# A hybrid decoder block: the SSD skip factors are loaded as one row per partition, and their column layout is formed on chip

## The chip, the cores and the metric

The kernel runs on one core of a Trainium2 chip. The metric is the device time of one execution in microseconds. A core has a matrix engine (PE), a vector engine (DVE), a scalar engine (ACT), a general engine (POOL) and a sync engine (SP), which here issues nearly all transfers. Each engine works through its own list of instructions in order, and an instruction that has to wait for another engine or for a transfer holds back everything behind it on its engine.

## The reference

One layer of a decoder for 512 tokens of width 1024, all in float32. After an RMSNorm, one projection of 11512 columns feeds three token mixers side by side: a sparse attention with a learned index (DSA), a three-way attention (NSA) and a state-space mixer (SSD). Their outputs are gated, mixed, projected and added to the input; a feed-forward block with squared ReLU follows.

```python
h = rms_norm(x, norm1_g)
u = h @ w_in
(dq, dk, dv, iq, ik, iw, nq, nkv, ng, sz, sxbc, sdt, mg) = split(u)
y_a, y_b, y_c = dsa(dq, dk, dv, iq, ik, iw), nsa(nq, nkv, ng), ssd(sz, sxbc, sdt)
x = x + (sig(g_A) * (y_a @ W_A) + sig(g_B) * (y_b @ W_B) + sig(g_C) * (y_c @ W_C)) @ w_out
x = x + square(relu(rms_norm(x, norm2_g) @ w_ff1)) @ w_ff2
```

The change touches one small constant, `ssd_d`: 32 skip factors, one for each head of the SSD. In the mixer they enter as

```python
y = y_diag + y_off + xs * d_skip.reshape(SSD_GROUPS, SSD_HPG)[:, :, None]
```

where `xs` has 32 heads of 64 channels, 2048 channels in all.

## The kernel before

A float32 product is made from split operands: each matrix is written as a high part in a reduced format and the remainder (`hTh` and `hTl` for the normalised input, `whi` and `wlo` for weights), and three matrix products are added (lines 458, 459 and 460). So every weight block goes through the same steps: SP loads 128x1024 floats into one of three buffers `wraw` (line 154), ACT makes `whi` (line 173), DVE or POOL makes `wlo` (line 175), which frees the `wraw` buffer for the next load, and PE uses both.

The start of the program matters here. The four token tiles of `x` are loaded, normalised, transposed on PE (line 427) and split into `hTh` by ACT (line 437) and `hTl` by DVE (line 438). While later tiles are still being made, PE begins the first projection, `c0`, 456 columns wide: for each token tile 24 products (lines 458 to 460), written to `pj` for tiles 0 and 1 and to `sc` for tiles 2 and 3. The transposes of token tiles 2 and 3 stand in the middle of this stream. The transposes of a tile write a buffer named `pT`, of which there are two; one is free again when line 438 has read it. The projection after `c0` is `nkv`, whose first four weight blocks are 128x1024.

Small constants are loaded by `const_load` (from line 322), which is called after token tile 1 of `c0` (line 705). A helper `wide` loads a row of n values once for each of the 128 partitions; `put` does the same into a tile that exists already, as for `dtb` and `alog`, the 32 step biases and decay logs of the SSD. The skip factors were different: the tile `dcol` has 128 partitions and 16 columns, and its element at partition p and column m is the factor of the head to which channel 128 m + p belongs, head 2m for p below 64 and head 2m + 1 above. It was filled by two loads, one for each half of the partitions, each taking every second of the 32 values (line 344), and halved in place on DVE (line 345). `const_cols` (from line 349) transposes other constants on PE and copies them; it is called after token tile 1 of `nkv` (line 742). `dcol` is first read by ACT in `conv`, line 860, when the SSD inputs are projected.

The order of the instructions on each engine is not that of the code: a scheduler places them by the order in which they are written, priorities, and a simulated timeline of its own. So an instruction that is written inside `const_load` can stand on DVE between two steps of the normalisation.

## Time and profile before

| what | value |
|---|---|
| median of 3 runs | 1374.2 us (1374.09 to 1375.94) |
| time of the profiled execution | 1373.8 us |
| its span, first to last instruction | 1372.1 us |
| mean granted clock of PE | 0.988 of full speed |
| PE busy | 1334.8 us, 97% of the span |
| DVE busy | 995.5 us, 73% |
| ACT busy | 727.6 us, 53% |
| POOL busy | 269.9 us, 20% |

The times in the prediction that come from the trace are counted from the start of the span. An engine counts as busy while it works on an instruction, not while it waits. In a line of the timeline the first two numbers are the start and the duration, then come the engine and the line of the program, what is written and from what, the shape, and in brackets the time that the engine sat idle before and what ended the wait. `SPq` is the queue of SP, where issuing a transfer is shown; when the data has landed stands in the view of the transfers. In the chain of waits each row is a start, a duration and what the end of the program was held by at that time.

### The profile page before, as it was taken

How to read it: one execution, taken by the hardware profiler on the slowest of the kernel's cores; microseconds unless marked ns; L12 is line 12 of the kernel's file. 1: busy time of each engine (PE TensorE's matmuls, PEld its weight loads, DVE VectorE, ACT ScalarE, POOL GpSimd, SP SyncE). 2: the span in 40 equal slices, each digit the busy share in tenths (PEclk: the TensorE clock that was granted, in tenths of full speed). 3: DMA queues.
4: the chain of work that ended last, by engine and by line, in shares of the span. 5: the costliest groups of instructions: out<-in, count | busy, mean ns of one | idle time of the engine just before them, and what ended most of it. 6: DMA issues, size and time to landing. Idle time of an engine off the chain costs nothing.

```text
span 1372.1 us, 19609 instructions
## 1 busy us (share of the span) xinstructions
PE 1334.8 (97%) x6827; PEld 1113.0 (81%) x6827; DVE 995.5 (73%) x1970; ACT 727.6 (53%) x1393; POOL 269.9 (20%) x242
## 2 busy tenths in 40 slices
PE   6899999999999999999999999999999999999998
PEld 5788888888887777888888888787879888888887
DVE  4469997788987767457768798979745666767741
ACT  4355525577777776347666655656334344444430
POOL 2135201111005667600000021113001201102000
PEclk8899999999999999999999999999999999999999
DMA  4335655555559999564336453434535655746531
GB/s 141 99 116 144 163 161 150 152 135 155 143 145 327 304 276 318 181 176 119 112 113 180 119 152 117 147 119 144 193 94 168 129 165 125 182 114 130 151 123 50
DMA packets 253713, 213.73 MB, mean 156 GB/s; under 512 B 17817, under 2 KB 205101, under 8 KB 253614
## 3 DMA queue, kind: packets, MB, share of 16 engines
q1 hardware_dynamic: 237644, 188.88, 45.9%
q0 software_dynamic: 15232, 20.98, 8.1%
q10 hardware_dynamic: 738, 2.63, 0.5%
q8 instruction: 54, 0.88, 0.3%
q14 instruction: 45, 0.37, 0.1%
HBM read 171.74 MB, written 40.70 MB: 155 GB/s over the span
## 4 chain that ended last, share of the span: by engine, by line
PE 82%; DMA 7%; DVE 6%; ACT 2%; issue 2%; POOL 1%; SPq 0%; DVEq 0%; ACTq 0%; POOLq 0%
PE pj L458 19%; PE pj L459 19%; PE pj L460 19%; PE sc L460 3%; PE sc L459 3%; PE sc L458 3%; PE pT L983 2%; DMA dcol<-in_ssd_d_dram 2%; PE sc L924 2%; PE sc L923 2%; PE pv L995 2%; PE pv L996 1%; PE sc L1311 1%; DMA yr<-yc_d 1%; DMA E<-ac_d 1%
## 5 line engine op out<-in xcount | busy, mean ns | idle before, releaser
L173 ACT ACTIVATE whi<-wraw 128x1024 fp32r<-128x1024 f32 (+2 forms) x190 | 198.3, 1047 | 256.9 <-PE pj L459 136.8
L175 DVE TENSOR_TENSOR wlo<-wraw,whi 128x1024 fp32r<-128x1024 f32 (+1 forms) x176 | 223.3, 1273 | 99.6 <-ACT whi L173 99.2
L458 PE MATMUL pj<-hTh,whi 128*128 128x512 f32 x512 | 203.7, 398 | 2.3 <-DVE cacc L852 2.0
L460 PE MATMUL pj<-hTh,wlo 128*128 128x512 f32 x512 | 202.6, 396 | 0.0
L459 PE MATMUL pj<-hTl,whi 128*128 128x512 f32 x512 | 202.4, 395 | 0.0
L932 ACT ACTIVATE p<-p,nb,rs 128x256 f32<-128x256 f32 (+3 forms) x160 | 107.8, 676 | 34.2 <-DVE nb L930 34.1
L458 PEld LDWEIGHTS pj<-hTh,whi 128*128 128x128 f32 x512 | 96.7, 189 | 21.8 <-ACT eab L1340 2.2
L460 PEld LDWEIGHTS pj<-hTh,wlo 128*128 128x128 f32 x512 | 96.7, 189 | 18.9 <-issue 0.2
L459 PEld LDWEIGHTS pj<-hTl,whi 128*128 128x128 f32 x512 | 96.5, 189 | 18.5 <-issue 0.2
L458 PE MATMUL pj<-yh,whi 128*128 128x512 f32 (+1 forms) x288 | 106.1, 373 | 4.1 <-ACT yh L828 3.1
L459 PE MATMUL pj<-yl,whi 128*128 128x512 f32 (+1 forms) x288 | 107.2, 372 | 0.1
L460 PE MATMUL pj<-yh,wlo 128*128 128x512 f32 (+1 forms) x288 | 106.1, 368 | 0.0
L459 PE MATMUL pj<-h2l,whi 128*128 128x512 f32 (+1 forms) x256 | 96.3, 376 | 0.0
L460 PE MATMUL pj<-h2h,wlo 128*128 128x512 f32 (+1 forms) x256 | 96.2, 376 | 0.0
L458 PE MATMUL pj<-h2h,whi 128*128 128x512 f32 (+1 forms) x256 | 96.1, 376 | 0.0
L458 PE MATMUL pj<-whi,hTh 128*128 128x512 f32 (+2 forms) x208 | 81.4, 391 | 3.2 <-DVE v_s L560 2.2
L460 PE MATMUL pj<-whi,hTl 128*128 128x512 f32 (+2 forms) x208 | 80.6, 388 | 0.0
L459 PE MATMUL pj<-wlo,hTh 128*128 128x512 f32 (+2 forms) x208 | 80.1, 385 | 0.0
L1042 POOL DMA_DIRECT2D qu<-q_d x32 | 23.6, 738 | 272.4 <-PE sc L924 165.5
L987 ACT ACTIVATE pth<-pT 128x512 fp32r<-128x512 f32 x95 | 54.9, 593 | 32.1 <-PE pT L983 28.6
L458 PE MATMUL sc<-whi,fh 128*128 128x512 f32 x168 | 65.4, 389 | 0.0
L459 PE MATMUL sc<-wlo,fh 128*128 128x512 f32 x168 | 65.4, 389 | 0.0
(408 smaller groups left out, 3159.5 us busy)
## 6 DMA issues: line engine op xcount, KB each, us to landing
wraw<-in_w_in_dram SPq DMA_DIRECT2D x84, 512.0 KB, 3.9
wraw<-in_w_ff_dram SPq DMA_DIRECT2D x58, 512.0 KB, 4.1
qd<-in_w_ff_dram POOLq DMA_DIRECT2D x18, 512.0 KB, 5.8
gld<-g_d SPq DMA_DIRECT2D x35, 256.0 KB, 2.7
q_d<-qev SPq DMA_DIRECT2D x64, 128.0 KB, 3.3
qu<-q_d POOLq DMA_DIRECT2D x32, 256.0 KB, 3.6
E<-ac_d SPq DMA_DIRECT2D x16, 512.0 KB, 6.7
xz<-xzt_d SPq DMA_DIRECT2D x16, 512.0 KB, 5.2
```

What stands on the lines that cost most here:

```text
L173: act.activation(hi[:, :m], r[:, :m], AF.Copy)
L175: (pool if i in LOWP else dve).tensor_tensor(lo[:, :m], r[:, :m], f(hi[:, :m]), op=ALU.subtract)
L458: pe.matmul(o, lh, rh, start=first, stop=False)
L459: pe.matmul(o, lh, rl, start=False, stop=False)
L460: pe.matmul(o, ll, rh, start=False, stop=last)
L923: pe.matmul(s_[:, h % w, :n], u.q[h], kh[:, :n], start=True, stop=False)
L924: pe.matmul(s_[:, h % w, :n], u.q[h], kl[:, :n], start=False, stop=True)
L932: act.activation(u.p[h][:, :n], u.p[h][:, :n], AF.Exp, bias=u.nb[:, h:h + 1], scale=rs8[:, u.b, u.h0 + h:u.h0 + h + 1], accum_out=u.sm[:, ...
L983: pe.transpose(pt[:, h], u.p[h][:, kb * 128:kb * 128 + 128], ident)
L987: act.activation(ph, ptf, AF.Copy)
L995: pe.matmul(o, vk, ph0, start=st, stop=False)
L1042: pool.dma_start(q.rearrange("p (i a) c -> p i (a c)", i=2), src)
```

## The change

The two strided loads of `dcol` and the halving in place go away. `const_load` loads the 32 factors as one contiguous row for every partition into a new tile `dsk`, as `wide` does for other constants. `const_cols` gets two DVE instructions, one for each half of the partitions: each reads every second column of `dsk`, multiplies by 0.5 and writes the 16 columns of `dcol`. The values in `dcol` are the same as before.

```diff
--- before.py
+++ after.py
@@ -340,9 +340,7 @@
         rows("posr", A["nsa_cmp_pos"], 64, 64)
         put(dtb, A["ssd_dt_bias"], 32)
         put(alog, A["ssd_a_log"], 32)
-        for e in range(2):
-            nc.sync.dma_start(dcol[64 * e:64 * e + 64], dram(A["ssd_d"], e, [[0, 64], [2, 16]]))
-        dve.tensor_scalar(dcol, dcol, 0.5, None, op0=ALU.mult)
+        wide("dsk", A["ssd_d"], 32)
         dve.tensor_tensor(g_dsa, CL["gq_d"], CL["gk_d"], op=ALU.mult)
         dve.tensor_tensor(g_nsa, CL["gk_n"].rearrange("p (a b) -> p a b", b=64), bc(CL["gq_n"][:, None, :], [128, 3, 64]), op=ALU.mult)
 
@@ -354,6 +352,9 @@
         pe.transpose(p[:, 184:200], CL["rows3"], ident[:16, :16])
         dve.tensor_copy(convc, p[:, 0:120])
         dve.tensor_copy(gcol, p[:, 184:200])
+        for e in range(2):
+            r = slice(64 * e, 64 * e + 64)
+            dve.tensor_scalar(dcol[r], CL["dsk"].rearrange("p (m e) -> p m e", e=2)[r, :, e], 0.5, None, op0=ALU.mult)
         pv_ = p[:64, 120:184].rearrange("p (v a l) -> p v a l", v=2, l=2)
         dve.tensor_copy(pos2[0:64], pv_[:, :, :, 0])
         dve.tensor_copy(pos2[64:128], pv_[:, :, :, 1])
```

How the lists of the engines read at the two places concerned, with line numbers of each kernel's own text (from `const_cols` on, a line of the changed kernel has a number higher by one). First DVE, at the end of the normalisation, before the change; `x_125` and `x_126` are token tiles 2 and 3, `wlo` 128x912 the last weight block of `c0`, and what stands after "waits" are the counters on which the instruction waits (those beginning with DMA are transfers).

```order
L438 TENSOR_TENSOR hTl<-pT,hTh 128x4x128 [waits Activation_49] x2
L412 SCALAR_TENSOR_TENSOR x_125<-x_125,rs_168,sc 128x512 [waits DMAHW3_49,Pool_49]
L412 SCALAR_TENSOR_TENSOR x_126<-x_126,rs_168,sc 128x512 [waits DMAHW4_49,Pool_49]
L175 TENSOR_TENSOR wlo<-wraw,whi 128x912 [waits DMAHW2_49,DMAHW1_49,Activation_49]
L345 TENSOR_SCALAR dcol<-dcol 128x16 [waits DMAHW3_49,DMAHW2_49]
L438 TENSOR_TENSOR hTl<-pT,hTh 128x4x128 [waits Activation_49] x2
L175 TENSOR_TENSOR wlo<-wraw,whi 128x1024 [waits DMAHW6_49,Activation_49]
```

The same place of DVE with the change:

```order
L439 TENSOR_TENSOR hTl<-pT,hTh 128x4x128 [waits Activation_49] x2
L413 SCALAR_TENSOR_TENSOR x_125<-x_125,rs_168,sc 128x512 [waits DMAHW3_49,Pool_49]
L413 SCALAR_TENSOR_TENSOR x_126<-x_126,rs_168,sc 128x512 [waits DMAHW4_49,Pool_49]
L175 TENSOR_TENSOR wlo<-wraw,whi 128x912 [waits DMAHW2_49,DMAHW1_49,Activation_49]
L357 TENSOR_SCALAR dcol<-dsk 64x16 [waits DMAHW2_49]
L357 TENSOR_SCALAR dcol<-dsk 64x16
L439 TENSOR_TENSOR hTl<-pT,hTh 128x4x128 [waits Activation_49] x2
L175 TENSOR_TENSOR wlo<-wraw,whi 128x1024 [waits DMAHW6_49,Activation_49]
```

Although the code has the two new instructions in `const_cols`, the scheduler puts them where the one instruction stood: one is replaced by two, and the first of them waits for one transfer in place of two.

Then the transfers of SP around the skip factors, before the change:

```order
L324 DMA posr<-in_nsa_cmp_pos_dram 64x64 [waits DMAHW7_49]
L324 DMA dtb<-in_ssd_dt_bias_dram 128x32 [waits DMAHW0_49]
L324 DMA alog<-in_ssd_a_log_dram 128x32 [waits DMAHW1_49]
L344 DMA dcol<-in_ssd_d_dram 64x16x1 [waits DMAHW2_49]
L344 DMA dcol<-in_ssd_d_dram 64x16x1 [waits DMAHW3_49]
L154 DMA wraw<-in_w_in_dram 128x2x512 [waits DMAHW4_49,DVE_49]
L154 DMA wraw<-in_w_in_dram 128x2x512 [waits DMAHW5_49,DVE_49]
```

And with the change:

```order
L324 DMA posr<-in_nsa_cmp_pos_dram 64x64 [waits DMAHW7_49]
L324 DMA dtb<-in_ssd_dt_bias_dram 128x32 [waits DMAHW0_49]
L324 DMA alog<-in_ssd_a_log_dram 128x32 [waits DMAHW1_49]
L324 DMA dsk<-in_ssd_d_dram 128x32 [waits DMAHW2_49]
L154 DMA wraw<-in_w_in_dram 128x2x512 [waits DMAHW3_49,DVE_49]
L154 DMA wraw<-in_w_in_dram 128x2x512 [waits DMAHW4_49,DVE_49]
```

Two transfers become one in the same place, with the shape of the one for `alog`. The two rows after it are the second and third weight blocks of `nkv`. Apart from these places, the engines' lists hold the same instructions in the same order.

## The prediction

> **What bounds the kernel now.** I read the page first: which engine is full, and in which slices it is not.

> ```profile
> span 1372.1 us, 19609 instructions
> PE 1334.8 (97%) x6827; PEld 1113.0 (81%) x6827; DVE 995.5 (73%) x1970; ACT 727.6 (53%) x1393; POOL 269.9 (20%) x242
> PE   6899999999999999999999999999999999999998
> ```

> PE is busy for 97% of the span; only the first two slices of 34 us are visibly short. What PE lacks is 1372.1 - 1334.8 = 37.3 us, and the waits of PE, summed over the whole run, say where most of it lies:

> ```profile
> PE pT L427 <- DVE hTl L438: 15.4, 1, 15.4
> PE pj L458 <- ACT yh L828: 3.1, 3, 1.2
> PE pj L458 <- DVE v_s L560: 2.2, 1, 2.2
> ```

> One single wait, the transposes of token tile 3 waiting for DVE, holds 15.4 us; the next cause has 3.1 us in three pieces. The chain of waits over the first 60 us follows it back:

> ```profile
> 17.60 22.15 DMA dcol<-in_ssd_d_dram
> ...
> 39.85 0.17 DVE dcol L345
> 40.02 0.60 DVE hTl L438
> 40.63 0.04 issue
> 40.67 1.12 PE pT L427 x4
> ```

> The transposes start when DVE has split the transposed tile 2; DVE does that when it has halved `dcol`; and that waits for the second strided load of `dcol`, issued at 17.60 and landed 22.15 us later, at 39.75. The DVE timeline shows what queues behind this wait, the ACT timeline when its next input was there:

> ```profile
> 20.79 1.10 DVE L175 TENSOR_TENSOR wlo<-wraw,whi 128x912 fp32r<-128x912 f32 x1
> 39.85 0.17 DVE L345 TENSOR_SCALAR dcol<-dcol 128x16 f32<-128x16 f32 x1 [17.96 <-DMA dcol<-in_ssd_d_dram]
> 39.93 1.28 DVE L438 TENSOR_TENSOR hTl<-pT,hTh 128x512 fp32r<-128x512 f32 x2
> ```

> ```profile
> 22.36 1.08 ACT L437 ACTIVATE hTh<-pT 128x512 fp32r<-128x512 f32 x2 [2.77 <-PE pT L427]
> ```

> DVE is free at 21.89 and idle for 17.96 us. The `hTl` instructions behind the wait need only `hTh`, whose two halves ACT had written by 23.44. So a constant that nobody reads before the SSD projections stops the normalisation, and through it PE.

> **The change part by part.** *The stall on PE.* These rows of PE's timeline carry the sum:

> ```profile
> 17.59 0.37 PE L458 MATMUL pj<-whi,hTh 128*128 128x456 f32 x1
> 20.08 0.36 PE L458 MATMUL pj<-whi,hTh 128*128 128x456 f32 x1
> 21.73 1.03 PE L427 MATMUL pT<-ident,x 128*128 128x128 f32 x8
> 22.52 0.46 PE L459 MATMUL pj<-wlo,hTh 128*128 128x456 f32 x1
> 24.89 0.36 PE L459 MATMUL sc<-wlo,hTh 128*128 128x456 f32 x1
> 40.67 1.12 PE L427 MATMUL pT<-ident,x 128*128 128x128 f32 x4 [15.42 <-DVE hTl L438]
> 46.15 0.90 PE L427 MATMUL pT<-ident,x 128*128 128x128 f32 x4
> 46.80 0.45 PE L460 MATMUL sc<-whi,hTl 128*128 128x456 f32 x1
> 53.92 0.39 PE L458 MATMUL pj<-whi,hTh 128*128 128x512 f32 x1
> 54.15 0.40 PE L459 MATMUL pj<-wlo,hTh 128*128 128x512 f32 x1
> ```

> Products overlap, so I count from start to start. From 17.59 to 20.08 lie 12 products: 2.49 us, 0.21 each. The last product before the stall starts at 24.89, so the next instruction could have started at 25.10. It started at 40.67: **15.57 us**.

> *The slow restart.* After the stall PE is not at full speed. The granted clock, in stretches:

> ```profile
> 27.00:28.00 1.00, 0.00 (x0) 0.00 (x0) 0.00 (x0) 0.00 (x0) 0.00 (x0) 1.00 0.05 0
> 30.00:40.60 10.60, 0.00 (x0) 0.00 (x0) 0.75 (x3) 0.00 (x0) 0.00 (x0) 0.50 0.24 77
> 45.00:46.00 1.00, 1.00 (x4) 0.88 (x3) 0.00 (x0) 0.00 (x0) 0.00 (x0) 0.50 0.10 37
> 47.00:48.00 1.00, 1.00 (x7) 0.91 (x6) 0.28 (x1) 0.92 (x4) 0.00 (x0) 1.00 0.00 0
> ```

> (The seventh number is the clock.) It was still 1.00 at 27 to 28, is 0.50 from 30 on, and stays there to 46, over five microseconds after work resumed. In this time PE does 4 transposes, 12 products and 4 transposes, from 40.67 to 46.80: 6.13 us. At full clock the same costs 2.49 us for the products and, from the row at 21.73 where 8 transposes take 22.52 - 21.73 = 0.79 us, 0.79 us for the transposes: 3.28 us. That is **2.85 us**, and it goes with the stall, provided PE finds its inputs: `pT` must be free at 25.10. [...]

> *The new load and the two DVE instructions.* No load of `dsk` is in the trace. The nearest rows, from the view of the transfers (number at the end: us from issue to landing; `dcol`'s is that of one of its loads), and SP's queue:

> ```profile
> wraw<-in_w_in_dram SPq DMA_DIRECT2D x5, 512.0 KB, 3.3
> gq_d<-in_dsa_q_norm_dram SPq DMA_DIRECT2D x1, 32.0 KB, 7.0
> dcol<-in_ssd_d_dram SPq DMA_DIRECT2D x2, 4.0 KB, 12.4
> alog<-in_ssd_a_log_dram SPq DMA_DIRECT2D x1, 16.0 KB, 2.9
> ```

> ```profile
> 16.42 0.43 SPq L324 DMA_DIRECT2D alog<-in_ssd_a_log_dram  x1
> 16.90 1.37 SPq L344 DMA_DIRECT2D dcol<-in_ssd_d_dram  x2
> ```

> `dsk` goes out at 16.90 in `dcol`'s place. `alog` has its shape, 128 rows of 32 floats from one address, was issued 0.48 us earlier on the same queue, and landed after 2.9 us. The lower bound is that; the upper one among row loads is `gq_d`, which went out beside the loads of `x` and took 7.0. So `dsk` lands between 19.8 and 23.9; I take 19.8, as `alog` is nearest in shape, queue and time. DVE comes to it at 21.89, so it does not wait. The two instructions cost at most 2 x 0.17 us (0.17 is the row of L345, on twice as many partitions), so DVE is free again at 22.23, before the first `hTh` at about 22.9: they are covered by the wait for ACT. Without that cover they would cost 0.17 us more than before on DVE and nothing on PE. `hTl` then takes 1.28 us from about 23.0 and has freed both `pT` buffers by 24.3, 0.8 us before PE asks. At the upper end, 23.9 + 0.34 + 0.68 = 24.9 frees the first buffer, still in time. So both ends give the same time.

> *The weights queued behind.* In the view of the transfers between 17 and 41 us stands:

> ```profile
> wraw<-in_w_in_dram SPq DMA_DIRECT2D x2, 512.0 KB, 21.1
> GB/s 351 46 20 4 0 0 0 0 0 0 0 0 0 0 0 0 0 0 0 0 0 0 0 0 0 0 0 0 0 0 0 0 0 28 144 202 246 376 294 195
> DMA packets 3014, 1.15 MB, mean 48 GB/s; under 512 B 2488, under 2 KB 2488, under 8 KB 3013
> ```

> Two weight blocks behind `dcol` took 21.1 us in place of 3.3: while 2488 small packets crept through, no bytes worth showing moved from 21 to 37. With one `dsk` of 128 rows ahead, the second block of `nkv` goes out near 17.4 and lands near 20.7; the third waits for the `wlo` that ends at 21.89 and lands near 25.2. PE enters `nkv` at 53.92 - 18.4 = 35.5, so they are early.

> *The sum.* 15.57 + 2.85 = **18.4 us**. What is late next? Everything after the `c0` products hangs on PE or on engines that PE feeds, and SP's next loads on buffers freed there, so I expect the rest, the 2.2 us wait at `v_s` included, to move earlier as one piece. The profiled execution took 1373.8 us around a span of 1372.1; 1373.8 - 18.4 = 1355.4. The median of the runs is 0.4 higher: 1374.2 - 18.4 = **1355.8 us**.

> **The rivals.** *The load stays late.* The order shows the two instructions on DVE at the old place; they are not later than before. If `dsk` needs the 12.4 us of one `dcol` load, it lands at 29.3, DVE delivers `hTl` at 29.3 + 0.34 + 0.6 = 30.2 and PE stands for 5.1 us. With the slow restart kept, that is a gain of 15.57 - 5.1 = 10.5: 1363.7 us. For it: same queue, same time. Against: `alog`. 6%.

> *The queue, not `dcol`, was slow.* If what silenced the transfers from 21 to 37 had another cause, the second block of `nkv` still lands at about 18.4 + 21.1 = 39.5. PE would use it six products after 35.5, at 35.5 + 6 x 0.23 = 36.9 (0.23 from the rows at 53.92 and 54.15), and stand until ACT (1.08) and DVE (1.28) have split it, taking the two-instruction rows as bounds: 41.9. That loses 5.0 us, and up to 2.85 for another slow restart: 1360.8 to 1363.7. Against: nothing else in this stretch has small packets in such number. 5%.

> *A later stall grows.* PE has 37.3 - 15.4 = 21.9 us of other gaps, some at transfers whose timing may fall differently. A tenth to a quarter of it is 2 to 5.5 us: 1358 to 1361.3. The waits listed are each short and tied to instructions that move along. 7%.

> *Slower.* `dsk` reads one address 128 times. If such reads were served one by one, DVE would be held until the last. It decides from a landing at 39.75, which is 22.85 us after issue or 0.18 us for each of 128 reads; at 0.20 us each it lands at 42.5 and the time is 1374.2 + 2.75 = 1377 us. Against it stands `alog` with the same reads in 2.9 us, 0.02 each. 2%.

> **How the numbers follow.** My forecast has 80%, 1352.5 to 1358: 18.4 with 2 to 3 us either way for stalls that shift. The range reaches over the smaller losses of the rivals, 1352.5 to 1360; outside it remain the late load, most of the slow queue, part of the later stall and the slower case. About 0.2%, 2.7 us, is what a measurement of this kernel can tell. Faster by more holds for all cases but the slower one and a rest that I have not thought of: 95%; the same 3%; slower 2%.

> **What would show it.** Right: DVE before the two `dcol` instructions idle for under 1 us; no 15 us wait in PE's list; PE's clock at 1.00 from 20 to 60 us; `nkv` starting at about 35.5; the two `wraw` loads landing after 3 to 5 us; the slices from the third on as before, moved. Wrong: a wait on `dsk`, an empty stretch of transfers after 20 us, or a span that falls by clearly less than the start of `nkv` moves.

## The result, and the profile after

The changed kernel takes 1356.5 us (median of four runs, 1355.3 to 1358.2); the kernel before, run beside it, took 1374.1. The ratio is 0.987 with a 95% interval of 0.9854 to 0.9886: 17.6 us less. The profiled execution took 1357.7 us around a span of 1356.0.

First the page of the changed kernel, then the waits of its PE, summed over the run (total, times, longest):

```profile
span 1356.0 us, 19609 instructions
PE 1333.3 (98%) x6827; PEld 1112.1 (82%) x6827; DVE 996.3 (73%) x1971; ACT 727.5 (54%) x1393; POOL 270.6 (20%) x242
PE   9999999999999999999999999999999999999998
```

```profile
PE pj L459 <- ACT yh L829: 3.3, 3, 1.4
PE pv L1312 <- issue: 2.4, 1, 2.4
PE pj L459 <- DVE v_s L561: 2.2, 1, 2.2
```

PE does the same work (1333.3 us busy against 1334.8); its gaps fell from 37.3 to 22.7 us, and the row of 15.4 us on `hTl` is gone. The first two slices, 6 and 8 before, are full. DVE's timeline at the place shows why:

```profile
20.08 1.10 DVE L175 TENSOR_TENSOR wlo<-wraw,whi 128x912 fp32r<-128x912 f32 x1
21.10 0.35 DVE L357 TENSOR_SCALAR dcol<-dsk 64x16 f32<-64x16 f32 x2
22.30 1.29 DVE L439 TENSOR_TENSOR hTl<-pT,hTh 128x512 fp32r<-128x512 f32 x2 [0.85 <-ACT hTh L438]
```

The two `dcol` steps start as soon as DVE is free, with no bracket for an idle time before them: `dsk` was there. They cost 0.35 us, inside the time in which DVE waits for ACT's `hTh` anyway. The queue behind `dsk` is as quick, in the view of the transfers from 12 to 41 us:

```profile
wraw<-in_w_in_dram SPq DMA_DIRECT2D x5, 512.0 KB, 3.4
```

Weight blocks land 3.4 us after issue, where two of them had taken 21.1. PE's timeline then has the transposes inside the stream of `c0`, the start of `nkv`, and one short stop later:

```profile
24.19 0.37 PE L460 MATMUL sc<-wlo,hTh 128*128 128x456 f32 x1
24.39 0.60 PE L428 MATMUL pT<-ident,x 128*128 128x128 f32 x4
...
34.77 0.39 PE L459 MATMUL pj<-whi,hTh 128*128 128x512 f32 x1
...
66.51 0.62 PE L459 MATMUL pj<-whi,hTh 128*128 128x304 f32 x1 [2.22 <-DVE v_s L561]
```

To see where time came from and where some went again, I took the same PE instruction in both profiled executions, by its number in PE's list, and subtracted the starts:

| PE instruction | before | after | lead |
|---|---|---|---|
| last `c0` product before the old stall | 24.89 | 24.19 | 0.70 |
| first product of `nkv` | 53.92 | 34.77 | 19.15 |
| first product behind the wait for `v_s` | 85.69 | 66.51 | 19.18 |
| a transpose 6 us later | 92.01 | 74.35 | 17.66 |
| two products in the SSD stretch | 450.14, 545.10 | 432.28, 528.22 | 17.85, 16.88 |
| one in the attention after it | 850.20 | 834.43 | 15.77 |
| one near the end | 1368.05 | 1351.86 | 16.19 |

From the stall's place come 19.15 - 0.70 = 18.45 us. Of the lead of 19.18 at `v_s` three later places take 3 us back. What happens at the first shows in the clock: 1.5 us are lost right behind the wait for `v_s`. What cost the other two, in the SSD stretch and after it, was not settled. The seventh number of a row in the view by stretches is the clock; first the kernel before, at its wait for `v_s`, then the changed kernel:

```profile
85.00:87.00 2.00, 1.31 (x9) 1.31 (x10) 1.86 (x7) 0.84 (x5) 1.75 (x2) 1.00 0.83 258
```

```profile
66.00:67.00 1.00, 0.49 (x2) 0.49 (x3) 0.97 (x5) 0.66 (x4) 0.93 (x1) 0.72 0.85 221
67.00:69.00 2.00, 2.00 (x10) 2.00 (x10) 1.57 (x6) 0.22 (x1) 1.23 (x2) 0.50 0.39 152
69.00:70.00 1.00, 1.00 (x6) 1.00 (x6) 0.66 (x1) 0.00 (x0) 0.00 (x0) 0.57 0.00 0
```

The wait is as long in both (2.24 and 2.22 us), but after it PE went on at full clock before the change and at half clock for 3.4 us after it. The last section comes back to this.

### The profile page after: what moved, and what is told of

Its sections match the earlier page's. It is cut to its first block, busy times and chain, and to the rows that moved or that the text cites. A ratio compares the mean times of both kernels' runs of the same rounds, so it can differ in the third digit from the quotient of the medians.

```text
span 1356.0 us, 19609 instructions
## 1 busy us (share of the span) xinstructions
PE 1333.3 (98%) x6827; PEld 1112.1 (82%) x6827; DVE 996.3 (73%) x1971; ACT 727.5 (54%) x1393; POOL 270.6 (20%) x242
## 4 chain that ended last, share of the span: by engine, by line
PE 85%; DVE 6%; DMA 4%; issue 2%; POOL 1%; ACT 1%; SPq 0%; DVEq 0%; POOLq 0%; ACTq 0%
PE pj L459 20%; PE pj L460 20%; PE pj L461 20%; PE sc L461 3%; PE sc L459 3%; PE sc L460 3%; PE pT L984 2%; PE sc L925 2%; PE sc L924 2%; PE pv L996 2%; PE pv L997 2%; PE sc L1312 1%; DMA yr<-yc_d 1%; DVE wlo L175 1%; ACT p L933 1%
## 5 line engine op out<-in xcount | busy, mean ns | idle before, releaser
L175 DVE TENSOR_TENSOR wlo<-wraw,whi 128x1024 fp32r<-128x1024 f32 (+1 forms) x176 | 222.5, 1269 | 98.7 <-ACT whi L173 98.3
L459 PE MATMUL pj<-hTh,whi 128*128 128x512 f32 x512 | 203.7, 398 | 2.0 <-DVE cacc L853 1.8
L460 PE MATMUL pj<-hTl,whi 128*128 128x512 f32 x512 | 202.4, 395 | 0.0
L459 PEld LDWEIGHTS pj<-hTh,whi 128*128 128x128 f32 x512 | 96.7, 189 | 21.5 <-ACT E L1345 2.0
L460 PEld LDWEIGHTS pj<-hTl,whi 128*128 128x128 f32 x512 | 96.6, 189 | 18.5 <-issue 0.2
L459 PE MATMUL pj<-yh,whi 128*128 128x512 f32 (+1 forms) x288 | 106.3, 374 | 4.5 <-ACT yh L829 3.3
L460 PE MATMUL pj<-yl,whi 128*128 128x512 f32 (+1 forms) x288 | 107.0, 372 | 0.1
L460 PE MATMUL pj<-h2l,whi 128*128 128x512 f32 (+1 forms) x256 | 96.3, 376 | 0.0
L459 PE MATMUL pj<-h2h,whi 128*128 128x512 f32 (+1 forms) x256 | 96.1, 376 | 0.0
L459 PE MATMUL pj<-whi,hTh 128*128 128x512 f32 (+2 forms) x208 | 82.2, 395 | 2.2 <-DVE v_s L561 2.2
L460 PE MATMUL pj<-wlo,hTh 128*128 128x512 f32 (+2 forms) x208 | 80.6, 388 | 0.0
L459 PEld LDWEIGHTS pj<-yh,whi 128*128 128x128 f32 x288 | 54.0, 189 | 14.5 <-ACT yh L829 4.2
L459 PE MATMUL sc<-whi,fh 128*128 128x512 f32 x168 | 65.4, 389 | 0.0
## 6 DMA issues: line engine op xcount, KB each, us to landing
wraw<-in_w_in_dram SPq DMA_DIRECT2D x84, 512.0 KB, 4.0
wraw<-in_w_ff_dram SPq DMA_DIRECT2D x58, 512.0 KB, 4.0
qd<-in_w_ff_dram POOLq DMA_DIRECT2D x18, 512.0 KB, 5.8
E<-ac_d SPq DMA_DIRECT2D x16, 512.0 KB, 7.0
xz<-xzt_d SPq DMA_DIRECT2D x16, 512.0 KB, 4.7
```

Of the source, the lines that this page charges most:

```text
L175: (pool if i in LOWP else dve).tensor_tensor(lo[:, :m], r[:, :m], f(hi[:, :m]), op=ALU.subtract)
L459: pe.matmul(o, lh, rh, start=first, stop=False)
L460: pe.matmul(o, lh, rl, start=False, stop=False)
```

## The experiments

In the recorded expectations A is my theory and B its rival. All kernels but one are the changed kernel with one edit; times are medians, ratios are to the kernel before run in the same series.

**The same kernel again.**

> The changed kernel once more, unaltered, to see what its times do from one execution to the next. Its four times so far are 1355.27, 1355.35, 1357.67 and 1358.15 us, with mean granted clocks of 0.997, 0.997, 0.994 and 0.995. Theory A (the short waits of PE are sometimes followed by a stretch of 3.4 us at half clock, sometimes not): the times follow the clock, about 1355.3 at 0.997 and about 1357.9 at 0.994 to 0.995; in a profile at 0.997 PE's clock stays at 1.00 behind the 2.2 us wait for v_s, and the products there take 0.30 us; at 0.994 they take 0.46. Theory B (the spread is something else, transfers for example): times of 1358 at 0.997 and of 1355 at 0.994 occur as well.

Five runs gave 1355.3 us (1354.7 to 1358.9), ratio 0.9858 [0.9836, 0.9880]. The profiled one had the half clock behind `v_s` again. The single times fall around 1355 and around 1358, but the mean clock of an execution does not order them: one at 0.994 took 1354.9, one at 0.992 took 1357.1, one at 0.994 took 1358.9. What makes the spread of 3 us stays open; differences under that between the end times of single profiles are not read below.

**One strided load put back, which nobody reads.** Behind `dsk` on SP's queue, 2048 pieces of 4 bytes, as many as the two old `dcol` loads together:

```diff
         wide("dsk", A["ssd_d"], 32)
+        junk = early.tile([128, 16], F32, name="junk")
+        nc.sync.dma_start(junk, dram(A["ssd_d"], 0, [[0, 128], [2, 16]]))
```

> The changed kernel with one more load on the sync queue, right behind that of dsk: the 32 factors' every second value, 16 for each of 128 partitions, into a tile that nobody reads. So 2048 pieces of 4 bytes stand on the queue where dcol's two loads had them, but no engine waits for them. It parts the two harms of the old loads. Theory A (two harms, the DVE wait and the weights held up behind the pieces): no stall at the transposes, DVE's dcol steps as in the changed kernel, but the second and third block of nkv land near 39.5; PE goes into nkv at about 34.8, does six products, and stands from about 36 to 42; with the slow restart the time is 1361 to 1366 us. Theory B (the pieces harm only whoever reads them): 1356.5 us, as the changed kernel.

1367.6 us (1364.2 to 1370.2, six runs), ratio 0.9941 [0.9920, 0.9961]: 11 to 12 us of the gain gone, though no instruction waits for this load. That is the part of the weights, and it is larger than A's 1361 to 1366 us. DVE, ACT and PE, from their timelines:

```profile
21.05 0.34 DVE L359 TENSOR_SCALAR dcol<-dsk 64x16 f32<-64x16 f32 x2
```

```profile
43.20 1.06 ACT L173 ACTIVATE whi<-wraw 128x1024 fp32r<-128x1024 f32 x1 [14.49 <-DMA wraw<-in_w_in_dram]
44.16 0.58 ACT L591 ACTIVATE iqs<-pj 128x512 fp32r<-128x512 f32 x1
```

```profile
46.26 1.23 PE L598 MATMUL pT<-identr,iqs 128*128 128x128 f32 x8 [10.44 <-DVE v_d L563]
```

`dcol` is made at 21.05 without a wait, the normalisation runs through, and PE reaches `nkv` early. There ACT waits 14.5 us for the second weight block. PE does not stop at the product that needs the block but sooner, at the transposes of `iqs`, since the copy of `iqs` (44.16) stands behind the waiting `whi` in ACT's list. DVE then still has `wlo`, `iqs` and `v_d` to make, and the last of them is what the row names.

**The kernel before, with only the halving moved.** The two strided loads stay; DVE halves `dcol` later, behind the column copies:

```diff
-        dve.tensor_scalar(dcol, dcol, 0.5, None, op0=ALU.mult)
...
-        dve.tensor_copy(gcol, p[:, 184:200])
+        gc_ = dve.tensor_copy(gcol, p[:, 184:200])
+        with tc.issue_after(getattr(gc_, "ins", gc_)):
+            dve.tensor_scalar(dcol, dcol, 0.5, None, op0=ALU.mult)
```

> The kernel before with one thing moved: the halving of dcol on DVE stands behind the copies of const_cols, near 60 us, in place of in the normalisation. Both strided loads stay where they are. That is half of the change alone. Theory A (two harms; the unread strided load cost 11 us through the weights that came late): no 15 us wait at the transposes, but ACT waits for the second block of nkv until about 40 to 43 us and PE stands some 10 us in nkv: 1365 to 1369 us. Theory B (DVE's wait is all): 1355 to 1358 us.

1366.5 us (1365.7 to 1369.6), ratio 0.9942 [0.9926, 0.9958]. The wait that the chain named is gone, and half of its time is back at another place:

```profile
PE pT L596 <- DVE v_d L561: 8.6, 1, 8.6
```

```profile
40.55 1.06 ACT L173 ACTIVATE whi<-wraw 128x1024 fp32r<-128x1024 f32 x1 [12.60 <-DMA wraw<-in_w_in_dram]
41.52 0.58 ACT L589 ACTIVATE iqs<-pj 128x512 fp32r<-128x512 f32 x1
```

So the change removed two stalls that lay over one another. Moving the consumer alone is worth 8.8 us, removing the small pieces from the queue as well brings the other 9 to 10.

**Half of the pieces, with a reader.** The lower half of `dcol` as before (1024 pieces, halved in place at the old point), the upper half from `dsk`:

```diff
         wide("dsk", A["ssd_d"], 32)
+        nc.sync.dma_start(dcol[0:64], dram(A["ssd_d"], 0, [[0, 64], [2, 16]]))
+        dve.tensor_scalar(dcol[0:64], dcol[0:64], 0.5, None, op0=ALU.mult)
...
-        for e in range(2):
+        for e in range(1, 2):
```

> The changed kernel with one of the two old strided loads back: partitions 0 to 63 of dcol are loaded strided, 1024 pieces, and halved in place, the other half comes from dsk. DVE waits at the old place for half the pieces. Theory A (the price is per piece): the strided load, issued near 16.7, lands about 11 to 12 us later, near 28 to 29; PE stands at the transposes of token tile 3 from 24.4 to about 30, and with the slow restart of up to 2.85 us the time is 1362 to 1365 us. Theory B (a strided load has a fixed price of some 20 us, whatever its number of pieces): 1371 to 1374 us. Theory C (DVE's wait was not what held PE): 1356.5 us.

1366.0 us (1364.6 to 1367.0), ratio 0.9929 [0.9906, 0.9952]. From the chain of waits and PE's waits:

```profile
16.92 14.36 DMA dcol<-in_ssd_d_dram
```

```profile
PE pT L430 <- DVE hTl L441: 8.0, 1, 8.0
```

The load landed 14.36 us after issue. Before the change the first of the two loads, with as many pieces, took 12.4 and the second, behind it, 22.15: the time grows with the number of pieces. With half of them about half of PE's wait is back, 8.0 us of 15.4. That is A, with both its numbers too low: it had the load land by 29 us, which it did at 31.3, and the time end at 1365.

**The same pieces from ACT's queue, and from POOL's.** The unread load again, but issued by ACT behind `hTh` of token tile 1, or by POOL behind the last of the four scale factors of the normalisation:

```diff
+        junk = early.tile([128, 16], F32, name="junk")
+        with tc.issue_after(HX[1][0]):
+            act.dma_start(junk, dram(A["ssd_d"], 0, [[0, 128], [2, 16]]))
```

```diff
+        junk = early.tile([128, 16], F32, name="junk")
+        with tc.issue_after(RS[3]):
+            pool.dma_start(junk, dram(A["ssd_d"], 0, [[0, 128], [2, 16]]))
...
```

(`HX[1][0]` is ACT's step; `RS` is a new list of POOL's four, filled in lines that are not shown.)

> As with the unread strided load on the sync queue, but this load, 2048 pieces of 4 bytes, is issued by ACT, on ACT's queue, after the hTh of token tile 1. The sync queue is that of the changed kernel. Theory A (pieces hold up only what stands behind them on their own queue): the weight blocks of nkv land 3 to 5 us after issue, and the time is 1355 to 1358 us, plus under 1 us for the issue on ACT. Theory B (pieces take up something that all transfers share): the blocks land late too and PE stands in nkv, 1361 to 1366 us.

> As with the unread strided load on ACT's queue, 2048 pieces of 4 bytes, but issued by POOL after its last step of the normalisation, near 17 us, on POOL's own queue, whose transfers are of another kind (software_dynamic in the queue table). On ACT's queue the pieces made dsk land after 14.7 us and the weight blocks after 17, though they stood on another queue. Theory A (the pieces of SP's and ACT's queues go through something that these two share and POOL's does not): dsk lands after 3 to 5 us, the blocks of nkv after 3 to 5, 1355 to 1359 us. Theory B (the pieces hold up the transfer engines themselves, whoever issues them): late as on ACT's queue, 1364 to 1368 us.

From ACT's queue it takes 1366.0 us (1364.9 to 1367.9), ratio 0.9931 [0.9907, 0.9955]; from POOL's 1367.0 (1364.2 to 1369.2), ratio 0.9941 [0.9921, 0.9962]. Both times A fell: SP's transfers came late although the pieces stood on another queue. B held for the weights and for the time, but that PE stands in `nkv` came true only with the load on POOL's queue. The view of the transfers from 15 to 45 us with the load on ACT's queue, and from 15 to 55 with it on POOL's:

```profile
wraw<-in_w_in_dram SPq DMA_DIRECT2D x3, 512.0 KB, 17.0
...
dsk<-in_ssd_d_dram SPq DMA_DIRECT2D x1, 16.0 KB, 14.7
```

```profile
q0 software_dynamic: 48, 0.01, 43.9%
...
wraw<-in_w_in_dram SPq DMA_DIRECT2D x4, 512.0 KB, 21.0
...
junk<-in_ssd_d_dram POOLq DMA_DIRECT2D x1, 8.0 KB, 26.3
```

With the pieces on ACT's queue, SP's `dsk` took 14.7 us and its weights 17.0. DVE felt the first, since `dcol` is made from `dsk` early, and held PE at the old place, the transposes of token tile 3. From DVE's timeline and PE's waits:

```profile
31.11 0.35 DVE L360 TENSOR_SCALAR dcol<-dsk 64x16 f32<-64x16 f32 x2 [10.79 <-DMA dsk<-in_ssd_d_dram]
```

```profile
PE pT L431 <- DVE hTl L442: 8.5, 1, 8.5
```

Behind that stall the late weights were still in time: PE has no wait for them. With the pieces on POOL's queue it was the other way round. PE has no wait at the transposes of token tile 3, the weights took 21.0, and PE stood in `nkv` for 4.8 us:

```profile
PE pj L464 <- ACT whi L173: 4.8, 1, 4.8
```

**The same bytes in rows.** 128 rows of 64 bytes from the same addresses, on SP's queue:

```diff
+        junk = early.tile([128, 16], F32, name="junk")
+        nc.sync.dma_start(junk, dram(A["ssd_d"], 0, [[0, 128], [1, 16]]))
```

> The changed kernel with an unread load at the place of the one with 2048 pieces, and with the same 8 KB: 16 neighbouring floats for each of 128 partitions, 128 pieces of 64 bytes. Theory A (the number of pieces is the price, at some 9.4 ns each): the load is over in 1.2 us beside its fixed time, the blocks of nkv land 3 to 5 us after issue, 1355 to 1358 us. Theory B (the price is that of many reads of a few addresses, or of the bytes): the blocks land late as with the 2048 pieces, 1364 to 1368 us.

1356.7 us (1356.1 to 1357.2), ratio 0.9867 [0.9850, 0.9883]: nothing lost, weights after 3.6 us:

```profile
wraw<-in_w_in_dram SPq DMA_DIRECT2D x4, 512.0 KB, 3.6
```

Both loads move 8 KB and read each address 128 times, so neither is the price; the number of pieces is. All pieces of these runs come from the same 128 bytes of memory. Whether single elements from addresses far apart cost as much was not tried.

**The `dcol` steps later still.** Made to follow the copy of `gcol` on DVE:

```diff
-        dve.tensor_copy(gcol, p[:, 184:200])
+        gc_ = dve.tensor_copy(gcol, p[:, 184:200])
         for e in range(2):
...
+            with tc.issue_after(getattr(gc_, "ins", gc_)):
...
```

> The changed kernel with the two dcol steps held back until the copies of const_cols, so that they are later on DVE, as the code has them; the one load of dsk is as it is. Theory A (the form of the load does it all; where the two steps stand does not matter once dsk is there in time): 1355 to 1358 us, and the 2.2 us wait at v_s longer by at most 0.35 us. Theory B (the steps at the old place still cost something): 1354 us or less.

1357.7 us (1355.6 to 1361.3), ratio 0.9877 [0.9858, 0.9896]: no different from the change. In the changed kernel the scheduler leaves the two steps at the old early point (21.10), and since `dsk` is there this does no harm. A's bound for the wait at `v_s` was missed: at the later place the steps ran beside a split of POOL and took 2.25 us in place of 0.35, and the wait was 2.86 us, 0.64 longer and not at most 0.35. The medians do not show it.

```profile
60.46 2.25 DVE L358 TENSOR_SCALAR dcol<-dsk 64x16 f32<-64x16 f32 x2
```

**The next wait, at `v_s`.** It comes from DVE, of whose instructions ahead of `v_s` two are slow while POOL splits weights: 1.91 and 2.60 us, where the next of the same lines take 0.48 and 0.42. In the changed kernel, DVE and then POOL:

```profile
60.31 1.91 DVE L895 SCALAR_TENSOR_TENSOR mask<-irelu,iwt,caus 128x256 f32<-128x256 f32 x1
62.33 0.48 DVE L895 SCALAR_TENSOR_TENSOR mask<-irelu,iwt,mask 128x256 f32<-128x256 f32 x1
62.73 2.60 DVE L534 TENSOR_TENSOR sqk<-u 128x256 f32<-128x256 f32 x1
...
65.90 0.42 DVE L534 TENSOR_TENSOR sqk<-u 128x256 f32<-128x256 f32 x1
```

```profile
59.54 2.40 POOL L175 TENSOR_TENSOR wlo<-wraw,whi 128x1024 fp32r<-128x1024 f32 x1 [0.56 <-POOL wlo L175]
62.38 2.67 POOL L175 TENSOR_TENSOR wlo<-wraw,whi 128x1024 fp32r<-128x1024 f32 x1 [0.44 <-ACT whi L173]
```

The slow `mask` and `sqk` end at 62.22 and 65.33, each 0.28 us after a POOL split (61.94 and 65.05). What ties their ends to those of the splits was not shown.

Two kernels give the last splits before `v_s` to DVE, which also changes the order in many later places:

```diff
-LOWP = {0} | set(range(8, 14)) | set(range(17, 24))
+LOWP = {0} | set(range(8, 12)) | set(range(17, 24))
```

> The changed kernel with one number altered: the low parts of weight blocks 12 and 13 are made by DVE and not by POOL. In the changed kernel two DVE instructions run beside those POOL splits and take 1.9 and 2.6 us in place of 0.5 and 0.4, after which PE waits 2.2 us for v_s and then, in some executions, works at half clock for 3.4 us. Theory A (POOL's splits beside DVE make the wait): both DVE instructions take 0.4 to 0.5 us, the wait at v_s and the half clock behind it are gone, and the time is 2 to 4 us below the changed kernel's 1355 to 1357: 1351.5 to 1354.5 us. Theory B (DVE is too full there: two more splits of 1.2 us on DVE give the time back): a wait of 1 us or more stays at the same place and the time is 1355 us or more.

The second does so for one block only, with `range(8, 13)`:

> The changed kernel with the low part of weight block 13 alone made by DVE and not by POOL. With blocks 12 and 13 on DVE the 2.2 us wait at v_s and the half clock behind it were gone (PE 3.6 us ahead at 66 us), but the scheduler then set other places differently and the lead was lost later, mostly in the NSA stage, between 630 and 924 us. Theory A (the lead is local and what comes later is the scheduler's luck): PE is 2 to 4 us ahead at 70 us; the end is anywhere between 1351 and 1360 us. Theory B (what one gains there is always taken back by the stage that the transfers bound): ahead at 70 us, and within 1 us of the changed kernel, 1355 to 1357, at the end.

1359.1 us (1357.3 to 1360.4), ratio 0.9884 [0.9869, 0.9898], and 1360.7 (1359.9 to 1361.7), ratio 0.9902 [0.9888, 0.9917]: 2.6 and 4.2 us above the changed kernel. With two blocks moved the local slowness is gone:

```profile
61.60 0.48 DVE L895 SCALAR_TENSOR_TENSOR mask<-irelu,iwt,caus 128x256 f32<-128x256 f32 x1
61.99 0.42 DVE L534 TENSOR_TENSOR sqk<-u 128x256 f32<-128x256 f32 x1
```

The wait for `v_s` is off PE's list, and PE is 3.6 us ahead of the changed kernel at 70 us. It is still 3.9 ahead near 600 us, and 0.7 behind from 1000 us on; in between the scheduler has chosen another order. That is neither what A nor what B said; which instruction costs it there was not settled. With block 13 alone moved, 1.0 us of the wait for `v_s` stays, PE is 1.8 us ahead at 70 us and 2.7 behind at the end, so both of its theories missed. That POOL's splits make the wait at `v_s` is shown; that removing them gains time is not, and 2.6 us lie within the spread of single runs. No kernel tried is faster than the changed one.

## Why the prediction was right

The time came out as predicted, 1356.5 against 1355.8, inside the likeliest case's own range, and by the predicted stall. That it came within 0.7 us is partly luck: single runs spread over 3 us, and in the profiled execution 3 us of the lead that PE had at `nkv` were gone at the end. By its steps:

- **What bounds the kernel.** Right as far as the chain goes: DVE's wait for `dcol` held PE. But the kernel before without that wait is only 8.8 us faster. A chain names the last arrival alone; the late weights lay under it.
- **The stall, 15.57, and the slow restart, 2.85.** Together 18.4; by the starts of the same instructions 18.45. `nkv` was predicted at 35.5 and starts at 34.77; the 0.7 us between them is a lead that was there before the stall's place. The 18.45 bears out the 2.85.
- **The load and the two DVE steps.** `dsk` was there by 21.10, at most 4.9 us after its issue at about 16.2; I had 2.9 with an upper bound of 7.0. The steps took 0.35 us, covered by the wait for ACT.
- **The weights behind.** Predicted back to about 3.3 us: 3.4. I named this part and gave it no price of its own, since nothing waited there. It is about half of the gain: with the wait of DVE gone and the pieces still there, only 8.8 us are won.
- **"The rest moves as one piece."** This step failed, by a small sum, and the prediction's own sign of it appeared: the span fell by 16.1 us where the start of `nkv` moved by 19.15. The `v_s` wait moved as it was, but PE restarted behind it at half clock, 1.5 us, and 1 us in the SSD stretch and 0.7 after it were lost in this execution: a lead of 16.2 us at the end, where the runs' medians have 17.6.
- **The rivals.** None decided the time. *The load stays late* is what happens when pieces are under way from another queue (10.8 us of wait, with the load on ACT's queue). *The queue, not `dcol`, was slow* was wrong in its cause, since `dcol`'s own pieces made the weights late, and its price was too small: I let PE stand for 5.0 us, from 36.9 to 41.9, and in the kernels where this stall occurs it stands 8.6 and 10.4 us. The block came later than 39.5 (ACT starts on it at 40.55 and 43.20), PE stopped sooner, at `iqs`, and DVE had `iqs` and `v_d` to make before PE went on. *A later stall grows* came true in small: the 3 us given back in the profiled execution are of its size, though the median lies below its 1358. *Slower*: `dsk` reads one address 128 times and was there 4.9 us after its issue at most, where this rival needed 25.6.

## What to carry to other kernels

A load that falls apart into single elements should be priced by its pieces and looked for as the cause of any late transfer issued behind it or beside it: 2048 pieces made SP's weight blocks take 15.7 us from SP's own queue, 17.0 from ACT's and 21.0 from POOL's, against 3.4. Loading whole rows and picking the columns on an engine costs here 0.35 us of hidden time. When the chain names one wait, ask what else was late at that moment: remove the wait alone, and it is the second latest that decides. And before pricing a late input, read the list of the engine that waits for it, since the delay passes to what stands behind it there: the copy of `iqs`, behind a `whi` that waited 14.5 us with the unread load on SP's queue, stopped PE before the late block itself did.

## What the hardware showed that I had not expected

**Pieces cost time that the transfer engines do not show.** In the kernel before, the transfers from 21 to 33 us are nothing but `dcol`'s:

```profile
DMA packets 1292, 0.01 MB, mean 0 GB/s; under 512 B 1292, under 2 KB 1292, under 8 KB 1292
...
q1 hardware_dynamic: 1292, 0.01, 4.7%
```

1292 pieces in 12 us are 9.3 ns each for the whole core, or 0.15 us per piece for each of the 16 engines that the view of the transfers counts if all take part, while the row shows these engines busy for 4.7%. With the pieces on POOL's queue the same work is shown as 43.9% of 40 us in 48 packets: for 2048 pieces about 0.14 us per piece and engine (0.439 x 40 x 16 / 2048), nearly the same price. So a low share of busy transfer engines did not mean here that another transfer could get through.

```profile
76.03 0.41 PE L459 MATMUL pj<-whi,hTh 128*128 128x304 f32 x1 [2.51 <-DVE v_s L561]
77.00:78.00 1.00, 1.00 (x7) 1.00 (x7) 0.71 (x3) 0.22 (x1) 0.76 (x1) 0.67 0.31 117
```

```profile
76.67 0.41 PE L462 MATMUL pj<-whi,hTh 128*128 128x304 f32 x1 [2.22 <-DVE v_s L564]
27.00:28.00 1.00, 0.00 (x0) 0.00 (x0) 0.00 (x0) 0.00 (x0) 0.00 (x0) 0.52 0.05 3
78.00:80.00 2.00, 2.00 (x17) 2.00 (x16) 1.68 (x6) 0.88 (x3) 0.40 (x1) 1.00 0.12 44
```

```profile
67.70 0.41 PE L460 MATMUL pj<-whi,hTh 128*128 128x304 f32 x1 [2.86 <-DVE v_s L562]
523.00:524.00 1.00, 0.97 (x6) 1.00 (x7) 1.00 (x2) 0.00 (x0) 0.00 (x0) 0.69 0.86 296
68.00:70.00 2.00, 2.00 (x16) 2.00 (x15) 1.60 (x6) 0.23 (x1) 1.43 (x2) 1.00 0.17 64
```

A clock of 0.67 over 77 to 78 puts the change to half speed at 77.34; 0.52 over 27 to 28 puts one at 27.04, and 14 windows later lies 74.83; 0.69 over 523 to 524 puts one at 523.38, and 134 windows earlier lies 66.0.

| kernel | PE idle at `v_s` | most of it in one window | clock of the next window |
|---|---|---|---|
| changed | 64.29 to 66.51 | 63.03 to 66.44: 2.15 | half |
| late halving | 73.52 to 76.03 | 73.93 to 77.34: 2.10 | half |
| load on ACT's queue | 74.45 to 76.67 | 74.83 to 78.24: 1.84 | full |
| later `dcol` steps | 64.84 to 67.70 | 66.0 to 69.4: 1.70 | full |
| before | 83.45 to 85.69 | 84.3 to 87.7: 1.4 | full |

In these five, half clock follows where 2.10 and 2.15 of the 3.41 us of one window are idle, and not where at most 1.84 are, wherever the wait itself begins and ends. So by these five the 1.5 us behind `v_s` hangs on where the grid lies, which no kernel here set. The windows of the kernel before and of the changed one bear this out, but the limit is not sharp. From 8 us on these two have 777 windows at full clock. None of the 770 with less than 1.6 us idle is followed by half clock. Of the seven others, six are: 1.99, 2.10 and 3.41 us idle before the change, 1.81, 2.42 and the 2.15 of the table with it. The seventh, with 1.63 us idle from 958.12 on before the change, is not. So between 1.6 and 1.9 us idle time alone does not decide: 1.81 has half clock behind it, and the 1.84 with the load on ACT's queue has not. In the kernel with the unread load on SP's queue stands a window with 1.80 of 3.41 us busy, 1.61 idle, and half clock after it:

```profile
428.18:431.59 3.41, 1.80 (x14) 1.09 (x9) 3.37 (x5) 2.12 (x5) 2.06 (x3) 1.00 0.99 327
431.60:435.00 3.40, 3.40 (x10) 2.63 (x9) 3.37 (x5) 3.39 (x6) 0.66 (x1) 0.50 1.01 268
```

The same grid explains the 2.85 us of the prediction. In the kernel before,

```profile
29.00:30.00 1.00, 0.00 (x0) 0.00 (x0) 0.00 (x0) 0.00 (x0) 0.00 (x0) 0.84 0.05 0
46.00:47.00 1.00, 1.00 (x6) 0.85 (x5) 0.00 (x0) 0.00 (x0) 0.00 (x0) 0.62 0.00 0
```

the slow stretch runs from 29.68 to 46.76, five windows. Work came back at 40.67, 0.75 us into the fourth, and that window did not end it; only the next, which was busy throughout, did. So PE worked 6.1 us at half speed. With the unread load on SP's queue it came back at 46.26, 0.4 us into a window, and that window did end it, at 49.30, after 3.0 us:

```profile
49.00:50.00 1.00, 1.00 (x5) 0.78 (x5) 0.60 (x1) 1.00 (x7) 0.67 (x1) 0.85 0.80 268
```

In these two the price of a restart hung on where in a window the work came back.
